# Openings of the four big stages: logarithm straight from PSUM, the norm's steps at higher priority, and two stages' first weights loaded into other buffers

## The chip, the cores and the metric

One core of one Trainium2 chip runs the whole forward pass in one launch. The metric is device time in microseconds (us), the median of several runs. "PE" is TensorE, "DVE" VectorE, "ACT" ScalarE, "POOL" GpSimd, and "SP" is SyncE, whose queue issues the transfers.

## The reference, cut to what matters

Two layers over 512 latent tokens with 256 context tokens ahead of them, width 1024. Layer 0 mixes tokens by grouped-query attention, layer 1 by a bidirectional Mamba-2 SSD; each layer ends in a gated feed-forward network (FFN). Ahead of each of the four sub-layers stands a root-mean-square norm with a shift and a scale:

```
def rms_norm(x, g):
    y = x * lax.rsqrt(jnp.mean(x * x, axis=-1, keepdims=True) + EPS)
    return y * g
def modulate(x, shift, scale):
    return x * (1 + scale) + shift
for i in range(DEPTH):                       # DEPTH = 2
    h = modulate(rms_norm(x, norm_mix_w[i]), ...)
    x = x + gate * (attention_mixer(h) if i == 0 else mamba2_mixer(h))
    h = modulate(rms_norm(x, norm_ffn_w[i]), ...)
    g, u = jnp.split(h @ w_up[i], 2, axis=-1)          # D_FF = 2816
    x = x + gate * ((jax.nn.silu(dwconv(g)) * u) @ w_down[i])
```

## The kernel before, in words

**Products.** Activations lie feature-major: 8 tiles of 128 features by tokens. Every operand of a big product is split into a high part (fp32r, rounded) and a low remainder, and `mm3` (L101 to L111) makes three matmuls of it: high by high (L108), high weight by low activation (L109), low weight by high activation (L111). A weight of 128x1024 is loaded by SP (`load_w`, L96), rounded by ACT (L85, the cast to `wh`) and its remainder taken by DVE (L87, `wl`); the three tiles come from one ring of ten buffers of that size, the tag `t4`, which all stages share.

**Openings.** An opening is the passage from a stage that updates `x` to the stage that reads its norm. The token ranges go one after the other: the context first (where it is still needed), then the first 256 latent tokens (lat0), then the last 256 (lat1). For each range the closing stage updates one feature tile of `x` after another (L874 in `down`, L1284 in `add_out`), and `Norm.sq` squares each on ACT (L338) and adds it up (POOL, for the last tile DVE: L344, L345). When a range is finished, `Norm.gen` makes its norm while the next range's products run: `rstd_rows` sums over the features by matmul (L244, tile `ss`), DVE turns the sums into mean + EPS (L247, `rsa`), ACT takes logarithm and exponential (L249, `rsy`, which is 1/sqrt), DVE corrects them by one Newton step (L251, L252, L254), PE transposes the root across the partitions (L266, `rsT`), and `modulated` forms the eight feature tiles: DVE scales (L294, `ht`), ACT shifts and rounds (L299 and L300, or L303, giving `hh`), and DVE (L304) or POOL (L301) takes the remainder `hl`. Tiles of ffn norms are called `..f`, those of the SSD's norm `..s`.

**First products.** The next stage's first two weights are multiplied by all ranges in `first_tiles`, into two PSUM tiles of tag `S` (`ps_first`; there are two such buffers). Its matmuls on the ranges that are ready run while the last range's norm is being made. For the SSD, `ps_first` holds the projection for the time steps and the first x tile; ACT empties the former (L1007, L1008) and so frees the buffer for the next product, `ps_in`.

**Order.** Apart from the start of attention, whose PE, ACT and DVE orders are written out by hand, a planner fixes each engine's order ahead of the run: it simulates the machine and gives a free engine the ready instruction that was traced first. A transfer or an operation is placed when its buffer is free in that simulation. On the chip each engine then works through its list in that order.

**Pools.** Most tiles that live for one stage come from that stage's own pool (`pa` attention, `pf` first FFN, `pt` SSD, `pg` second FFN), which is closed after the next stage's `first_tiles`; the next pool takes its place in memory. The ten `t4` buffers and the norm's results `hh`, `hl` stand in a pool that is never closed.

Of the kernel before, what the change touches and what calls it, by code (L numbers as in the profile page):

```python
# [7 lines left out]
P = 128  # L8
F32 = mybir.dt.float32
F32R = mybir.dt.float32r  # L10
AF = mybir.ActivationFunctionType
ALU = mybir.AluOpType
# [3 lines left out]
D = 1024  # L16
# [55 lines left out]
def t4(g, name, dt=F32):  # L72
    return g.p.tile([P, 1024], dt, tag="t4", bufs=10, name=name)
# [14 lines left out]
    return cast  # L88


def load_w(g, dram, lo_engine="dve", pin=False, after=None):

    st = t4(g, "wst")
    wh = t4(g, "wh", F32R)
    wl = t4(g, "wl", F32R)
    g.nc.sync.dma_start(st, dram)  # L96
    cast = split(g, st, wh, wl, lo_engine=lo_engine, pin=pin)
    if after:
        behind(g, cast, after)
    return wh, wl  # L100
# [132 lines left out]


def rstd_rows(g, sq, n, cols, width, name, bank):

    nc = g.nc
    c = cols.shape[-1]  # L240
    nt = n // P
    ps = bank(f"ss{name}")
    for t in range(nt):
        nc.tensor.matmul(ps[:, t * c : (t + 1) * c], sq[:, t * P : (t + 1) * P], cols, start=True, stop=True)  # L244
    small = lambda nm: g.p.tile([P, nt * c], F32, tag="rst", bufs=8, name=nm)
    a, y, u = small("rsa"), small("rsy"), small("rsu")
    nc.vector.tensor_scalar(a, ps[:, : nt * c], 1.0 / width, EPS, ALU.mult, ALU.add)  # L247

    for f in ((lambda: nc.scalar.activation(y, a, AF.Ln)), (lambda: nc.scalar.activation(y, y, AF.Exp, scale=-0.5))):  # L249
        follow(g, f()) if g.tables else f()  # L250
    nc.vector.tensor_tensor(u, y, a, ALU.mult)  # L251
    nc.vector.scalar_tensor_tensor(u, y, -0.5, u, ALU.mult, ALU.mult)  # L252
    if c == 1:
        nc.vector.scalar_tensor_tensor(a, u, 1.5, y, ALU.add, ALU.mult)  # L254
        root = lambda t: a[:, t : t + 1].broadcast_to([P, P])
    else:
        rb = t3(g, f"rb{name}", n=n)
        wide = lambda v: v.unsqueeze(2).broadcast_to([P, nt * c, P // c])
        nc.vector.scalar_tensor_tensor(rb.rearrange("p (a b) -> p a b", b=P // c), wide(u), 1.5, wide(y),
                                       ALU.add, ALU.mult)  # L260
        root = lambda t: rb[:, t * P : (t + 1) * P]
    yield BREAK
    for t0 in range(0, nt, 4):
        pt = bank(f"rsT{name}")
        for t in range(t0, min(nt, t0 + 4)):
            nc.tensor.transpose(pt[:, (t - t0) * P : (t - t0 + 1) * P], root(t), g.ident)  # L266
        yield (pt, t0 * P, min(n, (t0 + 4) * P))
# [55 lines left out]
class Norm:  # L323
# [7 lines left out]

    def sq(self, seg, x, m):

        i, a, b = seg
        nc = self.g.nc
        sq = t3(self.g, f"sq{self.name}", n=b - a)
        for ap, c0, c1 in parts(x[i][m], a, b):
            nc.scalar.activation(sq[:, c0:c1], ap, AF.Square)  # L338
        if m in (0, 6):
            self.acc[seg, m] = sq  # L340
            return
        acc = self.acc[seg, 6 if m == 7 else 0]
        if m == 7:
            nc.vector.tensor_tensor(acc, acc, self.acc[seg, 0], ALU.add)  # L344
        (nc.vector if m == 7 else nc.gpsimd).tensor_tensor(acc, acc, sq, ALU.add)  # L345

    def gen(self, seg, x, lag=2):

        i, a, b = seg
        g, nc, n = self.g, self.g.nc, b - a  # L350
        for _ in range(lag):
            yield
        rows = rstd_rows(g, self.acc[seg, 6], n, g.ones[:, :1], D, self.name, lambda nm: Bank(g, nm))
        next(rows)
        for _ in range(lag):
            yield
        rs = next(rows)[0][:, :n]
        for m in range(KT):
            modulated(g, self.h[i][m], x[i], rs, a, b, *self.a, self.streams[i][1], m,
                      pool=m in ((1, 4) if a else (1, 3, 5, 7)))  # L360
            yield


def gemm_in(g, tiles, h, off, segs):


    for run in segs:
        for ps, w in tiles:
            for k in range(KT):
                ks = slice(k * P, (k + 1) * P)  # L370
                mm3(g, (w[0][:, ks], w[1][:, ks]),
                    [(ps[:, off[i] + a : off[i] + b], tuple(t[:, a:b] for t in h[i][k])) for i, a, b in run],
                    k == 0, k == KT - 1)
                yield


def firsts(g, *units):
    return [load_w(g, u) for u in units]
# [507 lines left out]
def ffn(g, layer, streams, x, h, first, nxt=None, side=iter(()), after=()):  # L886

    nc, I = g.nc, g.I  # L890
    ns = len(streams)
    tot = sum(n for n, _ in streams)
    off = [0, L]

    cw = [g.par[:, PC[f"fw{layer}{t}"] : PC[f"fw{layer}{t}"] + NFT] for t in range(3)]
    cb = g.par[:, PC[f"fb{layer}"] : PC[f"fb{layer}"] + NFT]
    whole = [[(i, 0, n) for i, (n, _) in enumerate(streams)]]

    def gemm(t):

        if t % NFT == 0:
            ps = first[t // NFT]
        else:
            w = load_w(g, I["wup"][layer, t])
            if t % NFT == 1:
                out = []
                for i in range(ns):
                    ps = Bank(g, "ps_up1")
                    for _ in gemm_in(g, [(ps, w)], h, (0, 0), [[s] for s in whole[0] if s[0] == i]):
                        pass  # L910
                    out.append((ps, [i]))
                return [(ps[:, : streams[i][0]], off[i], off[i] + streams[i][0], i) for ps, (i,) in out]
            ps = S(g, "ps_up")
            for _ in gemm_in(g, [(ps, w)], h, off, [[s] for s in whole[0]]):
                pass
        return [(ps[:, :tot], 0, tot, None)]

    def up(f):
        pg = gemm(f)
        cv = t3(g, "cv", n=tot)  # L920
        w0, w1, w2 = (c[:, f : f + 1] for c in cw)
        for ps, a, b, _ in pg:
            nc.scalar.activation(cv[:, a:b], ps, AF.Identity, scale=w1, bias=cb[:, f : f + 1])
        for i in range(ns):
            a, b = off[i], off[i] + streams[i][0]
            ps, o = next((ps, o) for ps, o, e, j in pg if j in (None, i))
            nc.vector.scalar_tensor_tensor(cv[:, a + 1 : b], ps[:, a - o : b - o - 1], w0, cv[:, a + 1 : b], ALU.mult, ALU.add)
            nc.vector.scalar_tensor_tensor(cv[:, a : b - 1], ps[:, a - o + 1 : b - o], w2, cv[:, a : b - 1], ALU.mult, ALU.add)
        follow(g, nc.scalar.activation(cv, cv, AF.Silu))
        some = (2, 2, 2, 3)[f] if ns > 1 and f < 4 else 1  # L930
        for _ in range(some):
            next(side, None)
        pu = gemm(NFT + f)
        for _ in range(some):
            next(side, None)
        hd = t3(g, "hd", n=tot)
        for ps, a, b, _ in pu:
            nc.vector.tensor_tensor(hd[:, a:b], cv[:, a:b], ps, ALU.mult)
        hi, lo = t3(g, "hdh", F32R, n=tot), t3(g, "hdl", F32R, n=tot)
        split(g, hd, hi, lo)  # L940
        return [(hi[:, off[i] : off[i] + streams[i][0]], lo[:, off[i] : off[i] + streams[i][0]]) for i in range(ns)]

    gate = g.mod[layer][5]
    segs, f = [], 0
    for n in [3] + [2] * 8 + [3] if nxt else [2] * 11:
        segs.append(range(f, f + n))
        f += n
    acts, pend, wf = {}, None, []

    def flush(fs, order, norm=None, after=None):  # L950
        ws = [load_w(g, I["wdown"][layer, f * P : (f + 1) * P]) for f in fs]
        if after:
            wf.extend(firsts(g, *after))
        return down(g, ws, [acts.pop(f) for f in fs], gate, streams, x, order, norm, side=side)

    for fs in segs:
        for j, f in enumerate(fs):
            acts[f] = up(f)
            if j == 0 and pend:
                flush(pend, whole)  # L960
        pend = fs
    for _ in side:
        pass
    if nxt:
        ln_exp(g)
    return flush(pend, [[s] for s in ending(streams)], nxt, after), wf


def ssd(g, x, norm, wf, bg, close):
# [355 lines left out]
        for seg in SEGS[0]:  # L1325
            nxt.sq(seg, [xn], m)
    wt = [wm(m) for m in (6, 7)]
    wf = firsts(g, I["wup"][1, 0], I["wup"][1, NFT])
    bg = iter(())
    for seg in SEGS[0]:  # L1330
        _, a, b = seg
# [13 lines left out]
def body(nc, tc, I, out, dbg=None):  # L1345
# [21 lines left out]
                             ((CST_IDENT, CST_IDENT + P), (CST_BLK, CST_BLK + 2), (CST_SEL, CST_SEL + 2)))  # L1367
    g.ones = g.const.tile([P, P], F32, name="ones")
    nc.vector.memset(g.ones, 1.0)
    g.sc32 = g.const.tile([P, KT, 32], F32, name="sc32")  # L1370
    nc.vector.memset(g.sc32, 0.0)
    tc.keep_in_program_order(nc.scalar.preload_act_table_set("natural_log_exp_and_others"))
# [157 lines left out]
```

## Time and profile before

| what | us |
|---|---|
| median of 3 runs (1874.18 to 1875.43) | 1875.17 |
| profiled execution, its own time | 1875.38 |
| its span, first to last instruction | 1873.6 |
| PE busy in that span | 1848.9 |
| DVE busy | 1303.6 |
| ACT busy | 807.3 |
| POOL busy | 299.8 |

How to read it: PE is at work nearly all the time, so a change that adds or removes no matmul can move the time only through the stretches in which PE stands still or runs at half clock. The page leaves 1.78 us of the profiled execution outside the span.

### The profile page before, as it was taken

How to read it: one execution, taken by the hardware profiler on the slowest of the kernel's cores; microseconds unless marked ns; L12 is line 12 of the kernel's file. 1: busy time of each engine (PE TensorE's matmuls, PEld its weight loads, DVE VectorE, ACT ScalarE, POOL GpSimd, SP SyncE). 2: the span in 40 equal slices, each digit the busy share in tenths (PEclk: the TensorE clock that was granted, in tenths of full speed). 3: DMA queues.
4: the chain of work that ended last, by engine and by line, in shares of the span. 5: the costliest groups of instructions: out<-in, count | busy, mean ns of one | idle time of the engine just before them, and what ended most of it. 6: DMA issues, size and time to landing. Idle time of an engine off the chain costs nothing.

```text
span 1873.6 us, 28798 instructions
## 1 busy us (share of the span) xinstructions
PE 1848.9 (99%) x11474; PEld 1547.2 (83%) x11474; DVE 1303.6 (70%) x1950; ACT 807.3 (43%) x1402; POOL 299.8 (16%) x266
## 2 busy tenths in 40 slices
PE   9999999999999999999999999999999999999999
PEld 8876656798888888888888888888887888888887
DVE  6588888778787776544487787777797565565655
ACT  4534444363122222222367667776666352323231
POOL 2123120040000000000032333444443210000000
PEclk9999999999999999999999999999999999999999
DMA  9233151124444552211224432443352223222232
GB/s 345 76 109 101 63 178 52 57 84 164 146 135 145 191 185 99 68 58 56 68 91 141 124 105 87 124 124 113 124 178 93 79 91 97 95 95 97 90 103 89
DMA packets 74070, 211.67 MB, mean 113 GB/s; under 512 B 9040, under 2 KB 14544, under 8 KB 73808
## 3 DMA queue, kind: packets, MB, share of 16 engines
q1 hardware_dynamic: 73936, 209.84, 34.0%
q8 instruction: 90, 1.47, 0.3%
q14 instruction: 44, 0.36, 0.1%
HBM read 198.79 MB, written 6.82 MB: 110 GB/s over the span
## 4 chain that ended last, share of the span: by engine, by line
PE 84%; DVE 7%; issue 3%; DMA 2%; POOL 2%; ACT 2%; SPq 0%; DVEq 0%; POOLq 0%; ACTq 0%
PE ps_up L108 10%; PE ps_up L111 10%; PE ps_up L109 10%; PE ps_d L108 6%; PE ps_d L111 6%; PE ps_d L109 6%; PE ps_in L111 4%; PE ps_in L109 4%; PE ps_in L108 4%; PE ps_s L697 2%; PE ps_o L661 2%; PE ps_st L1123 2%; DMA wada<-in_adaA 1%; PE ps_wo L111 1%; PE ps_wo L108 1%
## 5 line engine op out<-in xcount | busy, mean ns | idle before, releaser
L87 DVE TENSOR_TENSOR wl<-wst,wh 128x1024 fp32r<-128x1024 f32 x207 | 258.5, 1249 | 233.9 <-PE ps_up L109 138.9
L85 ACT CAST wh<-wst 128x1024 fp32r<-128x1024 f32 x211 | 221.3, 1049 | 393.7 <-DMA wst<-in_wup 323.6
L108 PE MATMUL ps_up<-hhf,wh 128*128 128x512 f32 x1008 | 357.6, 355 | 0.0
L109 PE MATMUL ps_up<-hlf,wh 128*128 128x512 f32 x1008 | 357.3, 354 | 0.0
L111 PE MATMUL ps_up<-hhf,wl 128*128 128x512 f32 x1008 | 357.0, 354 | 0.0
L108 PEld LDWEIGHTS ps_up<-hhf,wh 128*128 128x128 f32 x1008 | 190.8, 189 | 26.4
L109 PEld LDWEIGHTS ps_up<-hlf,wh 128*128 128x128 f32 x1008 | 190.8, 189 | 26.3
L111 PEld LDWEIGHTS ps_up<-hhf,wl 128*128 128x128 f32 x1008 | 190.6, 189 | 26.4
L108 PE MATMUL ps_in<-hhs,wh 128*128 128x512 f32 (+1 forms) x560 | 204.4, 365 | 1.5 <-ACT dt L1008 1.5
L109 PE MATMUL ps_in<-hls,wh 128*128 128x512 f32 (+1 forms) x560 | 199.4, 356 | 0.0
L111 PE MATMUL ps_in<-hhs,wl 128*128 128x512 f32 (+1 forms) x560 | 198.7, 355 | 0.0
L108 PE MATMUL ps_d<-hdh,wh 128*128 128x512 f32 (+1 forms) x568 | 193.3, 342 | 0.2 <-ACT hdh L85 0.2
L111 PE MATMUL ps_d<-hdh,wl 128*128 128x512 f32 (+1 forms) x568 | 193.5, 341 | 0.0
L109 PE MATMUL ps_d<-hdl,wh 128*128 128x512 f32 (+1 forms) x568 | 192.9, 340 | 0.3 <-DVE hdl L87 0.3
L874 DVE SCALAR_TENSOR_TENSOR X<-ps_d,mod,X 128x512 f32<-128x512 f32 (+1 forms) x224 | 124.3, 583 | 35.9 <-PE ps_d L111 35.2
L108 PEld LDWEIGHTS ps_in<-hhs,wh 128*128 128x128 f32 x560 | 105.9, 189 | 16.6 <-ACT dt L1008 1.7
L109 PEld LDWEIGHTS ps_d<-hdl,wh 128*128 128x128 f32 x568 | 106.7, 188 | 14.8 <-DVE hdl L87 0.7
L111 PEld LDWEIGHTS ps_in<-hhs,wl 128*128 128x128 f32 x560 | 105.8, 189 | 14.7
L111 PEld LDWEIGHTS ps_d<-hdh,wl 128*128 128x128 f32 x568 | 106.6, 188 | 13.1
L108 PEld LDWEIGHTS ps_d<-hdh,wh 128*128 128x128 f32 x568 | 106.3, 188 | 13.4 <-ACT hdh L85 0.7
L109 PEld LDWEIGHTS ps_in<-hls,wh 128*128 128x128 f32 x560 | 106.0, 189 | 13.2
L700 ACT ACTIVATE pr<-ps_s 128x1024 f32<-128x1024 f32 x56 | 57.2, 1021 | 107.2 <-PE ps_s L699 107.2
(339 smaller groups left out, 3653.4 us busy)
## 6 DMA issues: line engine op xcount, KB each, us to landing
wst<-in_wup SPq DMA_DIRECT2D x88, 512.0 KB, 3.3
wada<-in_adaT SPq DMA_DIRECT2D x56, 512.0 KB, 3.3
wst<-in_win SPq DMA_DIRECT2D x48, 512.0 KB, 3.4
wst<-in_wdown SPq DMA_DIRECT2D x44, 512.0 KB, 3.5
E<-ad SPq DMA_DIRECT2D x64, 256.0 KB, 6.9
wada<-in_adaB SPq DMA_DIRECT2D x24, 512.0 KB, 4.1
ec<-ead SPq DMA_DIRECT2D x64, 128.0 KB, 5.6
wst<-in_wout SPq DMA_DIRECT2D x16, 512.0 KB, 3.3
```

What stands on the lines that cost most here:

```text
L85: cast = keep(nc.scalar.copy(hi, src))
L87: keep(eng.tensor_tensor(lo, src, _r(hi), ALU.subtract))
L108: mm(out, wh, ah, start=first, stop=False)
L109: mm(out, wh, al, start=False, stop=False)
L111: mm(out, wl, ah, start=False, stop=last)
L661: nc.tensor.matmul(po[S64[e], :n], v, pr[:, 512 * e + off : 512 * e + off + n], start=first, stop=last)
L697: nc.tensor.matmul(outs[e], kk[e][a][S64[e], k], b[S64[e], q], start=i == 0, stop=False)
L700: exps.append(nc.scalar.activation(pr, ps, AF.Exp))
L874: nc.vector.scalar_tensor_tensor(ap, o[:, c0:c1], gate[:, m, v : v + 1], ap, ALU.mult, ALU.add)
L1123: nc.tensor.matmul(ps[:, d * 256 : (d + 1) * 256], Bt[:, t * P : (t + 1) * P], xw[d][t], start=t == ts[0], stop=t == ts[-1])
```

## The change

1. In `rstd_rows`, ACT takes the logarithm of `sums / width + EPS` straight from the PSUM tile (scale and a constant tile `g.eps` as bias). DVE's mean + EPS is still made, after the two ACT steps in the trace order, for the Newton step. This holds for all norms, those of attention's queries and keys included.
2. In the openings (`Norm`), the square and sum of the last feature tile are traced as if 200 instructions earlier, and everything from the sums to the transposed root as if 400 earlier.
3. The first two weights of the SSD (`flush(..., after)`) go to buffers of the first FFN's pool `pf` that its side work (`ada_dve`) has done with: the three `wada` buffers, `junk` and `cb`. Before, they took `t4` buffers.
4. The first two weights of the second FFN go to `t2` buffers (128x512) of the SSD's pool `pt`, each weight loaded, rounded and split in two halves.
5. `gemm_in` takes a weight's block out of one tile or of a list of two.

```diff
-def load_w(g, dram, lo_engine="dve", pin=False, after=None):
-    st = t4(g, "wst")
-    wh = t4(g, "wh", F32R)
-    wl = t4(g, "wl", F32R)
+def load_w(g, dram, lo_engine="dve", pin=False, after=None, tiles=None):
+    st, wh, wl = tiles or (t4(g, "wst"), t4(g, "wh", F32R), t4(g, "wl", F32R))
+    if isinstance(st, list):
+        for i in range(2):
+            g.nc.sync.dma_start(st[i], dram[:, i * 512 : (i + 1) * 512])
+            split(g, st[i], wh[i], wl[i])
+        return wh, wl
...
-    nc.vector.tensor_scalar(a, ps[:, : nt * c], 1.0 / width, EPS, ALU.mult, ALU.add)
-    for f in ((lambda: nc.scalar.activation(y, a, AF.Ln)), (lambda: nc.scalar.activation(y, y, AF.Exp, scale=-0.5))):
+    sums = ps[:, : nt * c]
+    for f in ((lambda: nc.scalar.activation(y, sums, AF.Ln, scale=1.0 / width, bias=g.eps)),
+              (lambda: nc.scalar.activation(y, y, AF.Exp, scale=-0.5))):
         follow(g, f()) if g.tables else f()
+    nc.vector.tensor_scalar(a, sums, 1.0 / width, EPS, ALU.mult, ALU.add)
...
     def sq(self, seg, x, m):
+        if m < 7:
+            return self.square(seg, x, m)
+        with self.g.tc.high_priority(200):
+            self.square(seg, x, m)
...
-        next(rows)
+        with g.tc.high_priority(400):
+            next(rows)
         for _ in range(lag):
             yield
-        rs = next(rows)[0][:, :n]
+        with g.tc.high_priority(400):
+            rs = next(rows)[0][:, :n]
...
-            wf.extend(firsts(g, *after))
+            part = lambda dt: g.t3p.tile([P, D], dt, tag="wada", bufs=3, name="wada")
+            both = g.t3p.tile([P, 2 * D], F32R, name="cb")
+            wf.append(load_w(g, after[0], tiles=(part(F32), part(F32R), part(F32R))))
+            wf.append(load_w(g, after[1], tiles=(g.t3p.tile([P, D], F32, tag="junk", bufs=1, name="junk"),
+                                                 both[:, :D], both[:, D:])))
...
-    wf = firsts(g, I["wup"][1, 0], I["wup"][1, NFT])
+    two = lambda dt=F32R: [t2("wf", dt) for _ in range(2)]
+    wf = [load_w(g, I["wup"][1, t], tiles=(two(F32), two(), two())) for t in (0, NFT)]
...
+    g.eps = g.const.tile([P, 1], F32, name="eps")
+    nc.vector.memset(g.eps, EPS)
```

More of the change, by code (lines that the diff above doesn't have):

```diff
@@ L332, in sq, with square @@
     def sq(self, seg, x, m):
+        if m < 7:
+            return self.square(seg, x, m)
+        with self.g.tc.high_priority(200):
+            self.square(seg, x, m)
+    def square(self, seg, x, m):
         i, a, b = seg
@@ L369, in gemm_in @@
             for k in range(KT):
-                ks = slice(k * P, (k + 1) * P)
-                mm3(g, (w[0][:, ks], w[1][:, ks]),
+                mm3(g, tuple(parts(v, k * P, (k + 1) * P)[0][0] for v in w),
                     [(ps[:, off[i] + a : off[i] + b], tuple(t[:, a:b] for t in h[i][k])) for i, a, b in run],
```

## The prediction

> **What bounds the kernel now.** I read the page first, then busy time by stage, then PE's waits, and last the timeline around the longest of them.
>
> ```profile
> PE 1848.9 (99%) x11474; PEld 1547.2 (83%) x11474; DVE 1303.6 (70%) x1950; ACT 807.3 (43%) x1402; POOL 299.8 (16%) x266
> L87 DVE TENSOR_TENSOR wl<-wst,wh 128x1024 fp32r<-128x1024 f32 x207 | 258.5, 1249 | 233.9 <-PE ps_up L109 138.9
> L85 ACT CAST wh<-wst 128x1024 fp32r<-128x1024 f32 x211 | 221.3, 1049 | 393.7 <-DMA wst<-in_wup 323.6
> ```
>
> PE is busy 1848.9 of 1873.6 us, and the change takes no matmul away. So 24.7 us of idleness, and time at a lower clock, are all that can be won. The second view has one row per stretch: its start and end, its length, each engine's busy time, the granted clock after POOL's.
>
> ```profile
> core 0: us, PE busy (x) PEld busy (x) DVE busy (x) ACT busy (x) POOL busy (x), PEclk, DMA share, GB/s
> 380.00:425.00 45.00, 43.40 (x328) 41.10 (x328) 35.64 (x78) 28.79 (x63) 16.34 (x20) 1.00 0.29 106
> 925.00:975.00 50.00, 45.95 (x373) 44.09 (x372) 38.10 (x94) 31.46 (x76) 20.50 (x25) 1.00 0.26 92
> 1490.00:1520.00 30.00, 27.19 (x203) 25.66 (x203) 22.57 (x49) 14.97 (x34) 5.13 (x6) 0.94 0.22 74
> 276.32:279.73 3.41, 1.98 (x20) 1.10 (x22) 2.73 (x4) 1.75 (x2) 0.00 (x0) 1.00 0.04 17
> 1508.53:1511.94 3.41, 1.41 (x10) 0.97 (x9) 2.81 (x8) 0.87 (x3) 0.00 (x0) 1.00 0.00 0
> 1511.94:1515.36 3.42, 3.42 (x13) 2.98 (x12) 3.42 (x9) 3.42 (x9) 0.89 (x2) 0.50 0.00 0
> ```
>
> The first three are the openings of the first FFN, the SSD and the second FFN. PE idles 1.6, 4.05 and 2.81 us there, 8.5 together. In the third the clock matters as well: after 3.41 us in which PE was busy for only 1.41, it was granted 0.50 for the next 3.42, which costs half of that, 1.7 us. A stretch of the same length with 1.98 busy stayed at 1.00; so the edge lies between 1.41 and 1.98. The matmuls that wait in the three openings (total, times, longest):
>
> ```profile
> PE ps_first L109 <- POOL hls L301: 1.6, 2, 1.3
> PE ps_first L109 <- POOL hlf L301: 1.5, 2, 1.2
> PE ps_in L108 <- ACT dt L1008: 1.5, 1, 1.5
> PE ps_first L108 <- ACT hhf L303: 1.1, 1, 1.1
> PE rsTf L266 <- DVE rsa L254: 0.9, 1, 0.9
> PE ps_first L109 <- DVE hlf L304: 0.8, 1, 0.8
> ```
>
> First FFN: 1.5. SSD: 1.6 and 1.5. Second FFN: 1.1 + 0.9 + 0.8 = 2.8, and 1.7 for the clock. That makes 9.1 us within reach.
>
> **The change part by part.**
>
> *Second FFN, the last range's norm.* Its chain, from the sums to the first rounded tile:
>
> ```profile
> 1506.36 0.58 PE L244 MATMUL ssf<-ones,sqf 128*128 128x1 f32 x4
> 1506.98 0.16 DVE L247 TENSOR_SCALAR rsa<-ssf 128x2 f32<-128x2 f32 x1 [0.76 <-PE ssf L244]
> 1507.17 0.20 ACT L249 ACTIVATE rsy<-rsa 128x2 f32<-128x2 f32 x1 [1.41 <-DVE rsa L247]
> 1507.28 1.03 ACT L85 CAST wh<-wst 128x1024 fp32r<-128x1024 f32 x1
> 1508.22 0.20 ACT L249 ACTIVATE rsy<-rsy 128x2 f32<-128x2 f32 x1
> 1508.35 1.23 DVE L87 TENSOR_TENSOR wl<-wst,wh 128x1024 fp32r<-128x1024 f32 x1 [1.21 <-ACT wh L85]
> 1509.49 0.15 DVE L251 TENSOR_TENSOR rsu<-rsy,rsa 128x2 f32<-128x2 f32 x1
> 1510.09 0.43 PE L266 MATMUL rsTf<-cst,rsa 128*128 128x128 f32 x2 [0.88 <-DVE rsa L254]
> 1511.07 0.51 ACT L303 ACTIVATE hhf<-ht,mod 128x256 fp32r<-128x256 f32 x1 [2.65 <-DVE ht L294]
> ```
>
> The sums end at 1506.94, and the logarithm starts at 1507.17, when DVE has passed them on; read from PSUM it starts where `rsa` did, at 1506.98: 0.19 saved. Between logarithm and exponential lies a weight's cast, between exponential and Newton step a weight's remainder. Without them the exponential would follow the logarithm's 0.20 at once (0.85 sooner) and the Newton step the exponential's (1509.49 less 1508.42: 1.07 sooner). Together 2.1 us. What the edit does to these two weight steps no row shows: the norm already stands ahead of later weights in the trace order, and they got in because the next norm step was not ready at that instant. Ends: 0.19 won, if they get in again, and 2.1. I take 2.1, because a chain that starts sooner finds the cast's weight not yet landed: the cast ran right in the chain's first gap. PE, out of other work at 1509.2 (1510.09 less 0.88), would then get its first tile at 1511.58 less 2.1 = 1509.5, so 0.4 of the two waits' 2.0 stays: -1.6. With 0.4 idle the 3.41-us stretch is far above 1.98 busy, and the half clock goes: -1.7.
>
> ```profile
> 1502.57 1.46 DVE L87 TENSOR_TENSOR wl<-wst,wh 128x1024 fp32r<-128x1024 f32 x1
> 1503.96 0.96 DVE L304 SCALAR_TENSOR_TENSOR hlf<-ht,mod,hhf 128x256 fp32r<-128x256 f32 x1
> ```
>
> The 0.8 wait is for this remainder of the range before, which stands behind one more weight. An earlier root may bring it ahead of the weight or not; half, -0.4. Second FFN: -3.7.
>
> *The SSD's norm.* Here the lag sits in DVE's and ACT's lists:
>
> ```profile
> 957.37 0.50 PE L244 MATMUL sss<-ones,sqs 128*128 128x1 f32 x4
> 958.66 0.14 DVE L247 TENSOR_SCALAR rsa<-sss 128x2 f32<-128x2 f32 x1
> 958.68 3.43 POOL L301 TENSOR_TENSOR hls<-ht,hhs 128x256 fp32r<-128x256 f32 x3 [2.91 <-ACT hhs L300]
> 959.72 0.19 ACT L249 ACTIVATE rsy<-rsa 128x2 f32<-128x2 f32 x1
> 959.94 0.20 ACT L249 ACTIVATE rsy<-rsy 128x2 f32<-128x2 f32 x1
> 960.74 0.70 DVE L251 TENSOR_TENSOR rsu<-rsy,rsa 128x2 f32<-128x2 f32 x1
> 962.83 0.38 PE L266 MATMUL rsTs<-cst,rsa 128*128 128x128 f32 x2
> ```
>
> From the end of the sums (957.87) to the transposes pass 4.96 us, where the second FFN's chain above needs 3.15 with two weights in it and about 1.05 without. With priority the norm goes ahead of the range before's `ht`, `hh`, `hl` in both lists, so the root comes some 2 to 3 us sooner. Each range gains so, and the remainders on POOL, which PE waits for, with it. Ends: 0, or even a loss where a range's norm pushes back the previous range's remainders, and all 1.6. I take 1.6, since a lead of 2 us is more than the longest wait of 1.3. The first FFN has the same shape: -1.5.
>
> *The SSD's first weights in `pf`: an added wait.* Every access to the SSD's pool waits until `pf` is released:
>
> ```profile
> 969.99 0.47 DVE L304 SCALAR_TENSOR_TENSOR hls<-ht,mod,hhs 128x256 fp32r<-128x256 f32 x1
> 970.62 0.20 ACT L1000 ACTIVATE na<-par 128x1 f32<-128x1 f32 x1 [1.64 <-DVE hls L304]
> 971.56 0.57 ACT L1007 ACTIVATE dte<-ps_first,par 64x384 f32<-64x384 f32 x1 [0.74 <-PE ps_first L111]
> 971.96 0.28 PE L111 MATMUL ps_first<-hhs,wl 128*128 128x256 f32 x1
> 973.10 0.56 ACT L1008 ACTIVATE dt<-ps_first,par 64x384 f32<-64x384 f32 x1
> 973.71 0.38 PE L108 MATMUL ps_in<-hhs,wh 128*128 128x256 f32 x1 [1.47 <-ACT dt L1008]
> ```
>
> L1000 reads only parameters, yet it waits for the last `hl`, the last reader in `pf`. With weights in `pf` the last readers are the `ps_first` matmuls, which end at 972.24. Then come L1000 (0.20) and the four emptying steps (971.56 to 973.66: 2.1), so `ps_in` starts at about 974.6 where it was 973.71: +0.9. Behind L1000 in ACT's list stand the emptying steps, and for them waits PE, which has no other PSUM buffer of that kind. The idle stretch grows to 2.4 us, which leaves some 1.0 busy in 3.41, below the 1.41 that brought the half clock; where the 3.41-us grid cuts it in two, it stays above. I take the drop: +1.7. SSD: -1.6 + 0.9 + 1.7 = +1.0.
>
> By the Trainium skill, page "TensorE: Matmul & The Clock Gate", section "Why this matters for your kernels", the clock falls after idle gaps of over some 3 us. By it the 2.4 us would leave the clock alone, and the sum below would be 1.7 us lower. The rows differ: gaps of 0.88 and about 1.1 us within one 3.41-us stretch brought 0.50.
>
> *The rest.* Weights of the second FFN in `pt`: `pg`'s first tile then waits for the last `ps_first` too, but that only delays work which DVE and ACT (70% and 43% busy) owe PE later, while PE goes on with the next two weights; 0. Halves instead of wholes: between 0 more and, if a half cost as much as a whole, two casts and two remainders more (2 x 1.05 on ACT, 2 x 1.25 on DVE), ahead of the opening, beside 1.4 us or more of DVE slack in every 5; 0 of it on PE, up to 2.5 if that cover were gone. Two more transfers on SP likewise. The `t4` buffers that come free are taken by later weights, so the openings see as many weight steps as now; 0, and this is why I credit nothing to the early loading itself. The logarithm from PSUM in attention's ten norms shortens ACT's stand by some 0.2 us each, beside PE's work: 0. Memset of `g.eps`: 0.
>
> **The sum.** -3.7 - 1.5 + 1.0 = -4.2, against the profiled execution's own 1875.38: 1871.2. That stands 0.21 above the median of the runs, so 1871.0 as a median.
>
> **The rivals.**
> - *No clock drop at the SSD* (grid cuts the stretch, or the page's rule): 1871.0 - 1.7 = 1869.3. For it: the 2.4 us can fall 1.2 by 1.2. Against: the row with 1.41 busy.
> - *Weights slip into the second FFN's chain again*: only 0.19 of its 3.7 is won: 1871.0 + 3.5 = 1874.5. For it: priority cannot help a step that isn't ready, and the planner's clock isn't the chip's. Against: in the SSD's chain the exponential followed the logarithm by 0.03 us.
> - *Priority does nothing to the order* on the chip, and only the pool's wait shows: 1875.2 + 0.9 = 1876.1.
> - *Slower: the pool's wait decides.* Place: `ps_in` after the SSD's first products. Price: 0.9 + 1.7 = 2.6, so 1877.8 if the two FFN openings win nothing. It makes the kernel slower as soon as the three norms win less than 2.6 together. For it: the row of L1000. Against: it needs both FFN norms to stay as they are.
>
> **How the numbers follow.** A difference of 0.2% (3.75 us) is about what a measurement of this kernel tells from none. Chances: forecast 0.45, no drop 0.22, weights slip in 0.18, order unchanged 0.07, pool's wait decides 0.08. The forecast at 1871.0 lies almost on the bound of 1871.4; I count 0.3 of its 0.45 as faster by over 0.2%, the rest as within, and the rival at 1869.3 as faster. The two that end above 1874 count as within, and of the last I give 0.06 to beyond 1878.9 for reorderings in attention and SSD that no row prices. So 0.52 faster, 0.42 within, 0.06 slower. Range: down to all 9.1 won with the pool's wait and no drop (1875.2 - 9.1 + 0.9 = 1867.0), up to 1876.5, which takes in all but the last case; the forecast's own is 1868.5 to 1873.
>
> **What would show it.** Right: in the second FFN's opening no row at 0.50, and L249, L249, L251 one after another; in the SSD's, L266 within 3 us of L244; L1000 waiting for PE `ps_first`; `ps_in` waiting over 2 us for L1008, with 0.50 behind it. Wrong: L1000 still released by DVE; L85 or L87 between L249 and L251; new PE waits in attention or in the SSD's groups.

## The result, and the profile after

The changed kernel took 1886.09 us (median of 4 runs, 1885.67 to 1887.59) beside 1875.30 for the kernel before on the same chip: a ratio of 1.0061, 95% interval 1.0045 to 1.0077 (the ratios in this document are estimated from all runs of both kernels; they are not the quotients of the medians, here 1.0058). The prediction was 1871.0 in a range of 1867.0 to 1876.5, so the time lies outside, on the slower side. The page of the changed kernel:

```profile
span 1884.1 us, 28832 instructions
PE 1850.1 (98%) x11474; PEld 1547.3 (82%) x11474; DVE 1310.6 (70%) x1953; ACT 811.7 (43%) x1404; POOL 287.1 (15%) x266
```

PE's busy time is 1.2 us longer, the span 10.5. So PE stands still more. PE's waits (total, times, longest) say for what. The changed kernel and the experiments have other line numbers: L108, L109, L111 of `mm3` are now L111, L112, L114, the norm's steps lie 3 to 4 lines further down, the SSD's 16.

```profile
PE ps_xt L1113 <- DVE ec L1206: 10.0, 7, 1.9
PE ps_in L111 <- ACT dt L1024: 2.3, 1, 2.3
...
PE rsTf L270 <- DVE rsa L258: 1.5, 1, 1.5
```

The first row is new. `ps_xt` are the transposes of x in the SSD's eight groups of heads, a place that the prediction's sum gives nothing. In the kernel before, the same transposes waited 1.8 us in all, for another step:

```profile
PE ps_xt L1097 <- DVE xf L1200: 1.8, 6, 0.5
```

Two stretches, by window (columns as in the prediction): the groups' projections, from the first `ps_in` to the last, before and after; behind the second of them the openings of first FFN, SSD and second FFN after, and two stretches of 3.41 us out of the groups.

```profile
973.71:1396.81 423.10, 420.48 (x2477) 364.17 (x2478) 323.93 (x376) 291.74 (x617) 152.77 (x133) 1.00 0.39 119
```

```profile
973.89:1407.96 434.07, 422.38 (x2477) 364.90 (x2478) 330.93 (x375) 292.60 (x617) 142.10 (x133) 1.00 0.36 114
380.00:425.00 45.00, 44.41 (x329) 41.74 (x328) 39.72 (x82) 30.76 (x63) 14.60 (x19) 1.00 0.30 109
925.00:975.00 50.00, 45.25 (x363) 42.99 (x364) 38.75 (x93) 30.46 (x75) 18.74 (x25) 1.00 0.22 75
1500.00:1530.00 30.00, 27.23 (x209) 25.95 (x209) 21.89 (x49) 14.21 (x33) 5.85 (x6) 0.94 0.21 71
1225.70:1229.11 3.41, 1.47 (x10) 1.25 (x9) 3.15 (x5) 2.04 (x4) 0.14 (x1) 1.00 0.00 0
1229.11:1232.53 3.42, 3.42 (x10) 2.65 (x9) 1.39 (x2) 1.60 (x3) 1.16 (x2) 0.50 0.00 0
```

The same 2477 matmuls take 434.07 us instead of 423.10. PE idles 11.69 us there (434.07 less 422.38) instead of 2.62. PE's busy time is 1.9 longer, of which 1.7 is the half clock at 1229.11 behind one of the waits. So 11.0 us of loss lie in the groups. The openings moved the time by far less (the table below has them).

One such wait in detail, changed kernel, DVE first and then PE (start, duration, engine, line, tiles, count, idle time before it):

```profile
1052.95 1.21 DVE L87 TENSOR_TENSOR wl<-wst,wh 128x1024 fp32r<-128x1024 f32 x1
1054.08 1.01 DVE L1069 SCALAR_TENSOR_TENSOR Bf<-raw,par,Bf 128x770 f32<-128x770 f32 x1
1055.01 0.68 DVE L1206 TENSOR_TENSOR ec<-ec,ps_yo 128x512 f32<-128x512 f32 x1
```

```profile
1053.20 0.66 PE L1113 MATMUL ps_xt<-cst,xf 128*128 128x128 f32 x4
1055.74 0.66 PE L1113 MATMUL ps_xt<-cst,xf 128*128 128x128 f32 x4 [1.89 <-DVE ec L1206]
1056.15 0.49 PE L111 MATMUL ps_in<-hhs,wh 128*128 128x512 f32 x1
```

and the same place in the kernel before, PE:

```profile
1053.02 0.66 PE L1097 MATMUL ps_xt<-cst,xf 128*128 128x128 f32 x4
1053.43 0.47 PE L108 MATMUL ps_in<-hhs,wh 128*128 128x512 f32 x1
1053.75 0.39 PE L109 MATMUL ps_in<-hls,wh 128*128 128x512 f32 x1
1053.98 0.40 PE L111 MATMUL ps_in<-hhs,wl 128*128 128x512 f32 x1
1054.21 0.60 PE L1097 MATMUL ps_xt<-cst,xf 128*128 128x128 f32 x4
```

Before, PE's list has three `ps_in` matmuls between the first transposes and the second. After, the second transposes stand right behind the first, and the `ps_in` matmuls stand behind them. The first of these could have run: its weight had been cast by 1041.94, and ACT had emptied a PSUM buffer for it by 1053.23. The transposes need a PSUM buffer that DVE empties with `ec`. DVE has a weight's remainder and a convolution tap ahead of `ec`, and PE works in order, so it stands still.

Why the lists differ shows in SP's waits over the groups (985 to 1390 us): what each weight load waited for before it could be issued. Before:

```profile
SPq L96 <- DVE wl L87: 192.8, 29, 14.8
SPq L96 <- PE ps_in L111: 75.1, 12, 8.2
```

After:

```profile
SPq L99 <- PE ps_in L114: 213.2, 31, 13.1
SPq L99 <- PE ps_yo L1204: 42.9, 6, 8.3
SPq L99 <- DVE wl L87: 30.5, 3, 11.3
```

Each weight takes three of the ten `t4` buffers. Before, a load mostly waited for a buffer that DVE had read last; after, mostly for one that PE had read last. The loads, and with them casts and remainders, come at other times in each group. That the planner put the rest around them, and so moved the `ps_in` matmuls, is inferred from the lists; the planner itself left no trace.

### The profile page after: what moved, and what is told of

It is laid out like the page before. It is cut to its first block, busy times and chain, and to the rows that moved or that the text cites. A ratio compares the mean times of both kernels' runs of the same rounds, so it can differ in the third digit from the quotient of the medians.

```text
span 1884.1 us, 28832 instructions
## 1 busy us (share of the span) xinstructions
PE 1850.1 (98%) x11474; PEld 1547.3 (82%) x11474; DVE 1310.6 (70%) x1953; ACT 811.7 (43%) x1404; POOL 287.1 (15%) x266
## 4 chain that ended last, share of the span: by engine, by line
PE 77%; DVE 11%; issue 5%; ACT 3%; DMA 2%; POOL 2%; SPq 0%; POOLq 0%; DVEq 0%; ACTq 0%
PE ps_up L114 10%; PE ps_up L112 10%; PE ps_up L111 10%; PE ps_d L111 6%; PE ps_d L114 6%; PE ps_d L112 6%; PE ps_in L112 2%; PE ps_in L114 2%; PE ps_in L111 2%; PE ps_s L709 2%; DVE xf L1069 2%; PE ps_o L673 2%; DVE Bf L1069 1%; PE ps_wo L111 1%; PE ps_wo L112 1%
## 5 line engine op out<-in xcount | busy, mean ns | idle before, releaser
L87 DVE TENSOR_TENSOR wl<-wst,wh 128x1024 fp32r<-128x1024 f32 x203 | 250.2, 1233 | 306.9 <-PE ps_up L112 142.7
L85 ACT CAST wh<-wst 128x1024 fp32r<-128x1024 f32 x207 | 217.1, 1049 | 417.5 <-DMA wst<-in_wup 321.3
L112 PE MATMUL ps_up<-hlf,wh 128*128 128x512 f32 x1008 | 357.0, 354 | 0.0
L111 PE MATMUL ps_up<-hhf,wh 128*128 128x512 f32 x1008 | 356.9, 354 | 0.0
L114 PE MATMUL ps_up<-hhf,wl 128*128 128x512 f32 x1008 | 356.8, 354 | 0.0
L112 PEld LDWEIGHTS ps_up<-hlf,wh 128*128 128x128 f32 x1008 | 190.6, 189 | 26.4
L111 PEld LDWEIGHTS ps_up<-hhf,wh 128*128 128x128 f32 x1008 | 190.5, 189 | 26.4
L114 PEld LDWEIGHTS ps_up<-hhf,wl 128*128 128x128 f32 x1008 | 190.5, 189 | 26.4
L111 PE MATMUL ps_in<-hhs,wh 128*128 128x512 f32 (+1 forms) x560 | 205.0, 366 | 2.3 <-ACT dt L1024 2.3
L112 PE MATMUL ps_in<-hls,wh 128*128 128x512 f32 (+1 forms) x560 | 199.9, 357 | 0.0
L114 PE MATMUL ps_in<-hhs,wl 128*128 128x512 f32 (+1 forms) x560 | 199.3, 356 | 0.0
L114 PE MATMUL ps_d<-hdh,wl 128*128 128x512 f32 (+1 forms) x568 | 193.6, 341 | 0.0
L112 PE MATMUL ps_d<-hdl,wh 128*128 128x512 f32 (+1 forms) x568 | 193.2, 341 | 0.3 <-DVE hdl L87 0.3
L111 PE MATMUL ps_d<-hdh,wh 128*128 128x512 f32 (+1 forms) x568 | 193.1, 342 | 0.2 <-ACT hdh L85 0.2
L111 PEld LDWEIGHTS ps_in<-hhs,wh 128*128 128x128 f32 x560 | 106.3, 190 | 17.7 <-ACT dt L1024 2.5
L112 PEld LDWEIGHTS ps_d<-hdl,wh 128*128 128x128 f32 x568 | 106.7, 188 | 14.8 <-DVE hdl L87 0.7
L114 PEld LDWEIGHTS ps_in<-hhs,wl 128*128 128x128 f32 x560 | 106.1, 189 | 15.0
L114 PEld LDWEIGHTS ps_d<-hdh,wl 128*128 128x128 f32 x568 | 106.7, 188 | 13.1
L112 PEld LDWEIGHTS ps_in<-hls,wh 128*128 128x128 f32 x560 | 106.4, 190 | 13.5
L111 PEld LDWEIGHTS ps_d<-hdh,wh 128*128 128x128 f32 x568 | 106.3, 188 | 13.4 <-ACT hdh L85 0.6
```

The lines of the kernel that those rows point to most:

```text
L85: cast = keep(nc.scalar.copy(hi, src))
L87: keep(eng.tensor_tensor(lo, src, _r(hi), ALU.subtract))
L111: mm(out, wh, ah, start=first, stop=False)
L112: mm(out, wh, al, start=False, stop=False)
L114: mm(out, wl, ah, start=False, stop=last)
```

## The experiments

Theory A: the SSD's first weights no longer occupy six `t4` buffers, so the SSD's own weights get into the ring earlier and in another step with its buffers, and this sets other lists in the groups. Rivals: B, the pool's wait (which delays the groups' start) upsets them; C, the priorities or the logarithm do.

All runs in one table. The last three columns are stretches of the profiled execution, in us, between starts of matmuls: the SSD's opening (first `ps_first` to first `ps_in`), the groups (first `ps_in` to last `ps_y`), the second FFN's opening (last `ps_y` to its last `ps_first` matmul). The kernel before ran beside each group of experiments: its median was 1874.86 beside e1 to e4, 1874.05 beside e5 to e8, 1874.43 beside e9 to e12.

| kernel | median us | ratio to before (95%) | SSD opening | groups | 2nd FFN opening |
|---|---|---|---|---|---|
| before | | | 28.89 | 452.13 | 94.43 |
| after | 1886.09 | 1.0061 (1.0045-1.0077) | 29.98 | 463.91 | 93.11 |
| e1 SSD weights alone | 1888.45 | 1.0077 (1.0062-1.0092) | 29.43 | 466.13 | 92.84 |
| e2 all but SSD weights | 1874.82 | 0.9998 (0.9989-1.0007) | 27.98 | 452.08 | 93.97 |
| e3 = e2 + pool's wait | 1875.74 | 1.0009 (0.9999-1.0018) | 29.59 | 452.39 | 94.02 |
| e4 after, memsets in `t4` | 1884.95 | 1.0061 (1.0045-1.0078) | 29.72 | 468.60 | 92.50 |
| e5 after, `t4` held | 1873.57 | 0.9995 (0.9985-1.0004) | 27.96 | 452.92 | 93.20 |
| e6 FFN weights alone | 1874.35 | 1.0002 (0.9993-1.0011) | 28.93 | 452.09 | 93.67 |
| e7 logarithm + priorities | 1872.58 | 0.9996 (0.9986-1.0005) | 27.95 | 452.22 | 91.03 |
| e8 logarithm alone | 1874.66 | 1.0004 (0.9994-1.0013) | 29.36 | 452.20 | 90.59 |
| e9 = e2, `t4` held at FFN | 1872.18 | 0.9989 (0.9981-0.9998) | 28.13 | 452.32 | 90.95 |
| e10 e7 + SSD weights, held, no pool's wait | 1876.46 | 1.0008 (0.9999-1.0017) | 27.59 | 456.74 | 91.27 |
| e11 = e10 + FFN weights, held | 1876.29 | 1.0007 (0.9998-1.0016) | 27.59 | 456.14 | 91.35 |
| e12 priorities alone | 1874.90 | 1.0002 (0.9993-1.0011) | 28.93 | 452.14 | 93.89 |

Read the last two columns with the clock in mind: each stretch of 3.41 us at a granted clock of 0.50 lengthens them by up to 1.7. The last column holds one such stretch in before, after, e2 and e3, and none in the others; the groups hold one in after and e5, two in e4, e10 and e11, three in e1.

**e1 and e2: the SSD's weights alone, and all but them.** In e1 the rest of the change is undone; in e2 only this:

```diff
-            part = lambda dt: g.t3p.tile([P, D], dt, tag="wada", bufs=3, name="wada")
...
+            wf.extend(firsts(g, *after))
```

e1:

> The kernel before with one part of the change: the SSD's first two weights in pf instead of the t4 ring; logarithm, priorities and second FFN's weights as before. Theory A (six free t4 buffers let the SSD's own weights come earlier, so other steps stand in DVE's and PE's lists in its eight groups): the groups lose the 10 to 11 us that they lost in the full change, and nothing is won at the FFNs' openings: 1875.3 + 0.9 (the pool's wait) + 10.5 = about 1886.7, with ps_xt waiting for ec some 7 times, 10 us in all. Theory B (the pool's wait, which starts the groups 0.9 us later, upsets them): the same here. Theory C (the priorities or the logarithm upset the groups): 1875.3 + 0.9 = 1876.2, ps_xt waiting 2 us or less.

e2:

> The full change without that one part: the SSD's first weights stay in the t4 ring. Theories A and B: the groups run as before; what was won ahead of them and behind them in the full change stays: first FFN -1.5, second FFN's opening about -1.4, and no pool's wait (-0.7 by the start of ps_in): 1872 to 1873.5. Theory C: ps_xt still waits 10 us for ec, 1884 to 1886.

e1 lost the whole amount and a little more: groups 466.13 us, with the same row among PE's waits (`ps_xt` for `ec`, 10.4 us, 7 times). The little more goes with the clock: 0.50 for three stretches in e1's groups, for one in the changed kernel's. e2's groups took 452.08. Theory C falls. e2 was not the 1872 to 1873.5 that I expected but 1874.82; in the second FFN's opening it won 0.5 us, where e7 without the early weights won 3.4 (below).

**e3: the pool's wait alone.**

```diff
     ps_dt, ps_x0 = first_tiles(g, wf, norm, bg)
+    nc.vector.tensor_copy(g.t3p.tile([P, 1], F32, name="last"), ps_x0[:, T - 1 : T])
```

> The kernel of e2 with only the pool's wait put back: a DVE step of one element reads the last column of ps_first into a tile of pf before pf is released, so that the SSD's pool waits until the last ps_first matmul has ended, while the weights stay in t4. Theory A: ps_in starts 0.9 to 1.2 us later than in e2 and nothing else moves: e2 + 1, 1873 to 1874.5, ps_xt as before (about 2 us of waits). Theory B: the groups lose their 10 us: 1884 to 1886.

The SSD's opening grew by 1.6 us against e2 (27.98 to 29.59), the time by 0.9, which is within the noise; the groups stayed at 452.4. Theory B falls: the wait costs something in the opening and upsets nothing in the groups.

**e4 and e5: the buffers taken, and held.** Both are the full change. e4 takes six buffers for a memset each; e5 keeps them until the SSD's last `ps_first` (the added statements, each on a line of its own):

```diff
 # e4, in ssd, behind close()
+    [nc.gpsimd.memset(t4(g, "pad")[:, :1], 0.0) for _ in range(6)]
 # e5, in flush, behind the two loads
+            g.hold = [t4(g, "hold") for _ in range(6)]
+            [nc.gpsimd.memset(t[:, :1], 0.0) for t in g.hold]
 # e5, in ssd, behind first_tiles
+    [nc.vector.tensor_tensor(t[:, :1], t[:, :1], ps_x0[:, T - 1 : T], ALU.add) for t in g.hold]
```

e4:

> The full change, with six t4 buffers taken once (one memset of one column each on POOL, 6 x 0.1 us) where the SSD's weights would have taken them, behind the release of pf, so that the SSD's own weights come no earlier than before. Theory A: the groups' 10 to 11 us are gone, and the pool's wait is left: 1873 to 1875. Theory B and C: 1885 to 1887.

e5:

> The full change, with six t4 buffers held as long as the SSD's first weights held them before: six memsets of one column on POOL where those weights were loaded, and six DVE steps of one column behind the last ps_first. (In e4 each buffer was free again as soon as its memset had run, so e4 didn't hold them.) Theory A (the free buffers let the SSD's own weights come early, which sets the order of the eight groups): the groups run as in e3, without waits for ec; with the six steps and the pool's wait 1875 to 1877. Theory F (the order hangs on something else in that part, the pool pf's later end or the weights' own place): ps_xt waits 10 to 13 us for ec, 1884 to 1887.

e4 was a miss: 468.60 us in the groups, `ps_xt` waiting 13.1 us. Its buffers were free again as soon as each memset had run, so it did not hold back what theory A says must be held back; by itself it would also have fitted theory F. SP's timeline shows it. Counted from the SSD's first `ps_first`, the SSD's own first two weights are issued 8.5 and 11.0 us after it in the kernel before, 30.3 and 22.0 us ahead of it in the changed kernel, and 29.3 and 21.9 ahead in e4. In e5 they come 8.3 and 10.4 us after it, as before, and e5 decides. With everything else of the change in place the groups took 452.92 us, the time fell from 1886 to 1873.6, and the transposes' waits, and in the same window as above SP's, are nearly those of the kernel before:

```profile
PE ps_xt L1113 <- DVE xf L1216: 1.8, 6, 0.5
```

```profile
SPq L99 <- DVE wl L87: 192.4, 29, 14.8
SPq L99 <- PE ps_in L114: 82.0, 13, 8.3
```

So the loss hangs on when the six buffers come free. One rival is weakened but not excluded: the hold's small steps stand in the planner's lists too, and no run has those steps without the hold. Against it speak e4, whose six memsets turned nothing, and e9 below, where a hold works at another place. e5 shows a second thing. The stretch from the SSD's first to its last `ps_first` took 25.35 us, where after took 27.37 and e7, without the early weights, 27.28. Only with the buffers held did the early weights bring their 2 us there. The time does not show them: 1873.57 beside 1874.05 is within the noise.

**e6 and e7: what takes the gain at the second FFN.** e6 is before with the second FFN's weights in `pt` alone; e7 is the change with both pairs of weights back in `t4`.

> The kernel before with the second FFN's first two weights alone loaded early, in halves, in pt. Theory D (these free buffers put the norm's sums and its transposes close together in PE's list, ahead of the ps_wo products that could fill the gap): rsTf waits 1.5 us, with the clock at 0.5 behind it, and nothing else changes: 1875 to 1876.5. Theory E (the raised priority of the transposes does that): rsTf waits 0.9 us or less here, 1874 to 1875.

> The change's logarithm and priorities, with both pairs of first weights in the t4 ring as before. Theory D: rsTf waits 0.9 us or less, no row at 0.5 in the second FFN's opening, and its other waits are shorter by the priority: e2's 1874.8 less 1.5 to 3, 1872 to 1873.3. Theory E: rsTf waits 1.5 us as in e2, 1874.5 to 1875.

e7's opening took 91.03 us, e2's 93.97; the only difference there is the early weights. In the changed kernel one sees how they cost it. PE:

```profile
1506.00 0.50 PE L247 MATMUL ssf<-ones,sqf 128*128 128x1 f32 x4
1506.36 0.36 PE L112 MATMUL ps_wo<-yl,wh 128*128 128x256 f32 x1
1506.56 0.28 PE L114 MATMUL ps_wo<-yh,wl 128*128 128x256 f32 x1
1508.34 0.43 PE L270 MATMUL rsTf<-cst,rsa 128*128 128x128 f32 x2 [1.50 <-DVE rsa L258]
1508.53 0.36 PE L111 MATMUL ps_wo<-hhy,wh 128*128 128x256 f32 x1
```

and the 3.41-us stretches around it:

```profile
1505.60:1509.01 3.41, 1.91 (x17) 1.71 (x17) 1.58 (x8) 1.42 (x3) 0.00 (x0) 1.00 0.48 177
1509.01:1512.43 3.42, 3.42 (x19) 3.42 (x18) 3.42 (x9) 2.98 (x8) 0.80 (x2) 0.50 0.16 61
```

The first range's transposes stand two matmuls behind their sums, and the `ps_wo` products that could fill the 1.5 us stand behind the transposes; a half clock followed, another 1.7. e6 has the same wait, 1.3 us, without any priority, and e7 none with all of them. So it is theory D, not the priorities (E), that holds, although e6 had no row at 0.50 and lost nothing in all. Of the 2.9 us between e2 and e7 in this opening 1.7 are the half clock and 1.3 idle time of PE.

**e8: the logarithm alone**, and **e12: the priorities alone.**

> Logarithm from PSUM alone. By the prediction's terms 0 in attention and 0.2 to 0.4 in the second FFN: 1874.5 to 1875. Theory G (attention's norms are in PE's way, since in the three kernels of this study with the logarithm attention's scores took 247.6 to 247.8 us from the first to the last, where before had 248.7): attention a further 0.9 shorter, 1873.5 to 1874.

> The priorities alone. By the difference of e7 and e8: ps_in starts 0.7 us behind the SSD's last ps_first (before 1.75, e8 1.99), and nothing elsewhere; by the prediction 1.6 us for the SSD and 1.5 for the first FFN's opening (55.94 us from attention's last scores to the last ps_first before; 55.24 in e7, 56.22 in e8: 0.7 so far): 1 to 2 us under before. In the second FFN, where e8 alone has 90.59 us against 94.43: about 94 if the logarithm did all of it there.

e8's chain in the second FFN's last range:

```profile
1507.80 0.26 ACT L251 ACTIVATE rsy<-ssf,eps 128x2 f32<-128x2 f32 x1 [1.22 <-PE ssf L247]
1508.09 0.20 ACT L252 ACTIVATE rsy<-rsy 128x2 f32<-128x2 f32 x1
1508.20 1.03 ACT L85 CAST wh<-wst 128x1024 fp32r<-128x1024 f32 x1
```

```profile
1508.09 0.16 DVE L254 TENSOR_SCALAR rsa<-ssf 128x2 f32<-128x2 f32 x1 [1.05 <-ACT rsy L251]
1508.36 0.16 DVE L255 TENSOR_TENSOR rsu<-rsy,rsa 128x2 f32<-128x2 f32 x1
```

The cast stands behind the exponential, no remainder ahead of the Newton step: the chain that the prediction drew, and the opening fell from 94.43 to 90.59. Of these 3.8 us 1.7 are the half clock and 1.75 idle time of PE (3.20 before, 1.45 in e8). In e12 the half clock is gone too, but PE idles 3.50 us and the opening fell by 0.5 only. So in the profiles the logarithm did it alone. e12 also missed its forecast elsewhere: `ps_in` starts 1.87 us behind the last `ps_first`, not 0.7, and nothing was won in all.

By the timing both kernels are level with before: e8's interval, 0.9994 to 1.0013, leaves room for a gain of 1.1 us at most. The profiled execution of e8 was the fastest of its ten (1872.75 beside a median of 1874.66), and over all runs its mean granted clock was 0.9985, where the kernel before had 0.9986: it did not have fewer half clocks. A half clock that is missing from one profile is no gain of the kernel.

**e9 to e11: the buffers held at the second FFN too, and the pool's wait removed.** e9 is e2 with a hold as in e5, behind the second FFN's weights, read behind its `first_tiles`. e10 is e7 with e5's early SSD weights and hold, and with edits of which these are the main lines, so that nothing ahead of `ps_in` touches `pt`; two of the six held buffers take the first results of the time step's emptying. e11 adds e9's part:

```diff
-    na = small("na", [P, 1])
+    na = g.const.tile([P, 1], F32, name="na")
...
+    e0, r0 = (t[:, :TH] for t in g.hold[:2])
...
-        nc.scalar.activation(e[hs], src, AF.Abs, bias=par("dtb", 0)[hs])
-        nc.scalar.activation(dt[hs], src, AF.Relu, bias=par("dtb", 0)[hs])
+        nc.scalar.activation(e0[hs], src, AF.Abs, bias=par("dtb", 0)[hs])
+        nc.scalar.activation(r0[hs], src, AF.Relu, bias=par("dtb", 0)[hs])
```

> The kernel of e2 (logarithm, priorities, second FFN's weights early) with six t4 buffers held until the second FFN's last ps_first, by six one-column memsets on POOL and six one-column DVE steps. In e2 the stretch from the SSD's last ps_y to the second FFN's last ps_first took 93.97 us, in e7 without the early weights 91.03. Theory A (it is again the freed t4 buffers, filled by later weights whose steps move the opening's order): 91 or less, rsTf waits 0.6 us or less, e2 less 3: some 1.5 us under before. Theory H (the halves, or pt as their place, cost it): 93.5 to 94, as e2.

> Logarithm, priorities and the SSD's first weights in pf, with six t4 buffers held as in e5; two of the six are used for the first results of the time step's emptying (dte, dt), and na lies in the const pool, so that nothing in front of ps_in waits for pf. Second FFN's weights as before. e5's opening (25.35 us from the SSD's first to its last ps_first, where e7 took 27.28) with e7's 0.7 us to ps_in (e5: 2.61): 1.9 us less than e7, some 3.5 us under before. If the pool's wait isn't what the 2.61 is, 0 against e7.

> e10 with the second FFN's weights early too and their six buffers held as in e9: by theory A e10's time less up to 1.5 us (the opening of the second FFN without its weight steps), some 4 to 5 us under before; by theory H 3 us more than e10.

e9 bore out theory A a second time: 90.95 us for the opening instead of 93.97, and the only ratio of the study whose interval lies below 1 (0.9981 to 0.9998). Its median is 2.2 us under before. That is weak evidence for a gain: it is one interval out of thirteen, it just misses 1, and it overlaps e7's (0.9986 to 1.0005). e7 without early weights took 91.03 in that opening, so the early weights themselves add nothing. e10 and e11 were misses. With the pool's wait gone, PE waited for the weight instead:

```profile
970.36 0.38 PE L111 MATMUL ps_in<-hhs,wh 128*128 128x256 f32 x1 [2.98 <-ACT wh L85]
973.69 0.58 PE L114 MATMUL ps_in<-hhs,wl 128*128 128x256 f32 x1 [2.82 <-DVE wl L87]
```

The cast of that weight ran at 969.27, behind the emptying of `ps_first`: 5.8 us of new waits. They also cost clock:

```profile
969.30:972.71 3.41, 0.50 (x2) 0.30 (x2) 3.27 (x3) 2.89 (x4) 0.00 (x0) 1.00 0.00 0
972.71:976.12 3.41, 2.43 (x11) 2.43 (x12) 3.31 (x7) 0.00 (x0) 0.00 (x0) 0.50 0.00 0
976.12:979.54 3.42, 3.42 (x16) 3.23 (x15) 3.31 (x5) 0.00 (x0) 0.00 (x0) 0.50 0.00 0
```

With 2.43 us of PE busy in the first stretch at 0.50, the loss to the clock is 1.2 there and 1.7 in the second. The mean granted clock of e10's runs is 0.9962 where the kernel before has 0.9986, so this is not the profiled execution alone. e10 came out at 1876.46, e11 at 1876.29.

## Why the prediction was wrong, step by step

*The step that failed* is in "The rest": "The `t4` buffers that come free are taken by later weights, so the openings see as many weight steps as now; 0". The sentence was true and the price wrong: it looked at the openings alone, while the ring serves the groups too. Later weights did take them, and the SSD's opening gained nothing by the early ones (27.37 us to its last `ps_first`, e7 27.28). But the loads then followed the ring in another step through all eight groups, and there the term measured +11.8 us (463.91 less 452.13): 9.1 of idle time and 1.9 of busy time up to the last `ps_in`, 0.8 behind it. The prediction's text has the groups only as "0.06 to beyond 1878.9 for reorderings in attention and SSD that no row prices", and among its signs of being wrong, "new PE waits in attention or in the SSD's groups", which is the sign that came. A view that bore on it was there before the change: SP's waits, with 29 loads in the groups held up by DVE's remainders. The change touched just what they wait for. Why the planner's two patterns each keep themselves up through eight groups, no run here shows.

*The gains were too large as well.* The measured median lies 15.1 us above the forecast, and in the profiles the groups make up 11.8 of them. The rest are gains that did not come. For the logarithm and the priorities alone the prediction's terms give -3.7 - 1.5 - 1.6 = -6.8. That is e7, whose median lies 1.5 under before, with an interval of 0.9986 to 1.0005, so 2.6 us at most. (e7's profiled execution is 4.4 us shorter than before's from the first scores to the last matmul, 1754.4 for 1758.8; that this is near the sum of -4.2 is chance, since -4.2 also holds the early weights, which e7 lacks.)

*Second FFN, -3.7.* In the profiles the logarithm alone brings the two things that the prediction named, shorter waits and no half clock: -3.8 in e8, -3.4 in e7. But 1.7 of that is the half clock of one profiled execution, and e8's timing shows no gain, so the size is not borne out. In the change 2.9 of it went again (e2 against e7), for which the prediction had no term: the early weights were to cost 0. "Halves" and "`pg`'s first tile" were not the reason, since e9, with both, has 90.95. Two smaller slips in the working move nothing: 1509.5 less 1509.2 leaves 0.3 us of waiting, not 0.4, and the DVE slack of 1.4 us in every 5 holds for 1380 to 1490 us (1.5) but not for 1490 to 1504 (0.9).

*First FFN, -1.5.* PE's idle time in the window fell from 1.6 to 0.6 us, so -1.0; by the matmuls' starts, from attention's last scores to the last `ps_first`, 55.94 became 55.22. Right in kind, half to two thirds of the size; the priorities did it (54.91 in e12, 56.22 in e8).

*SSD's norm, -1.6.* Wrong. From the end of the sums to the transposes passed 4.96 us before. With the priorities, e12:

```profile
957.95 0.61 PE L247 MATMUL sss<-ones,sqs 128*128 128x1 f32 x4 [0.35 <-DVE sqs L356]
963.47 0.43 PE L270 MATMUL rsTs<-cst,rsa 128*128 128x128 f32 x2 [0.30 <-DVE rsa L258]
```

963.47 less 958.56, the end of the sums, is 4.91: nothing won. e7's DVE list shows why: between two steps of the chain, each of which waits for ACT's or its own last result, a ready step slips in.

```profile
959.21 0.67 DVE L256 SCALAR_TENSOR_TENSOR rsu<-rsy,rsu 128x2 f32<-128x2 f32 x1
959.80 1.21 DVE L87 TENSOR_TENSOR wl<-wst,wh 128x1024 fp32r<-128x1024 f32 x1
960.94 0.70 DVE L258 SCALAR_TENSOR_TENSOR rsa<-rsu,rsy 128x2 f32<-128x2 f32 x1
```

The prediction had that argument ("priority cannot help a step that isn't ready") for the second FFN, where it wasn't needed, and not here, where it was. What logarithm and priorities did win here together lies elsewhere: `ps_in` starts 0.67 us behind the last `ps_first` in e7, where it was 1.75 before; neither part alone brought it (1.99 in e8, 1.87 in e12).

*The pool's wait, +0.9.* Right against the kernel before: from the last `ps_first` to `ps_in` 1.75 us became 2.61. Against e2, which has 0.68 there, it is 1.9, since the wait also took back what the other parts had won. In the changed kernel L1016, the old L1000, waits for `ps_first` as foretold, and `ps_in` 2.33 us:

```profile
971.64 0.20 ACT L1016 ACTIVATE na<-par 128x1 f32<-128x1 f32 x1 [3.14 <-PE ps_first L114]
```

*Clock drop there, +1.7.* It fell out: the stretch was cut by the grid, as the rival at 1869.3 had it (1.85 and 2.63 us of PE busy; the rows are in the last section). The grid can be worked out from the rows: in the changed kernel the half clocks begin at 1229.11 and 1509.01, 279.90 us or 82 times 3.413 apart, and 973.11 lies 75 times 3.413 ahead of 1229.11. In e5 the same 2.3 us fell into one stretch, 1.08 us of PE busy, and brought 0.50:

```profile
969.18:972.59 3.41, 1.08 (x10) 1.08 (x10) 2.39 (x16) 3.25 (x8) 0.00 (x0) 1.00 0.56 189
972.59:976.01 3.42, 3.42 (x19) 3.42 (x18) 3.11 (x3) 3.20 (x6) 0.00 (x0) 0.50 0.30 121
```

By the Trainium skill, page "TensorE: Matmul & The Clock Gate", section "Why this matters for your kernels", the clock falls after idle gaps of over some 3 us. The rows differ, as those of before did: here it fell after a wait of 2.3 us, and at the second FFN after one of 1.5.

*The SSD's sum, +1.0,* came out by luck. The SSD's opening grew by 1.1 us in the profiles (28.89 to 29.98), but of the three terms -1.6, +0.9 and +1.7 only the middle one was there.

*Attention, 0.* The ten profiles with the logarithm need 247.6 to 248.9 us from the first scores to the last, the four without it 248.7, 249.0, 250.3 and 250.4. The slowest of the ten (e9) and the last two of the four (e1, e12) hold a half clock there. With 1.7 taken off for it, the ten lie at 247.2 to 248.1 and the four at 248.6 to 249.0. So the logarithm seems to win somewhat under a microsecond, for which the prediction had 0; the medians don't show it.

*The rival on the slower side* named the wrong place: the pool's wait cost its 0.9 and did not decide the time.

## What to carry to other kernels

Buffers set free are a change to every stage that shares their ring, not only to the one that gave them up: ask first what each later load waits for (the DMA queue's own waits), and allow for lists made by a planner to settle into another pattern. Here that pattern cost 11.8 us. Loading early without taking up a shared ring can be tried with the ring's buffers held for as long as before, which here turned 1886 into 1873.6 us. Raising the priority of a chain moves steps that are ready; the gaps between its dependent steps are still filled by others. And when two profiles differ by a half clock, look at the granted clock of all runs before counting it as won or lost.

## What the runs showed of the hardware that was not expected

The edge that the prediction drew for the clock, between 1.41 and 1.98 us of PE busy in a 3.41-us stretch, is no sharp one in this view. A stretch with 1.91 (1505.60, above) was followed by 0.50, and in the same run this one with 1.85 was not:

```profile
969.70:973.11 3.41, 1.85 (x17) 1.66 (x15) 0.60 (x8) 1.46 (x4) 0.00 (x0) 1.00 0.02 5
973.11:976.52 3.41, 2.63 (x22) 2.63 (x23) 1.75 (x4) 3.36 (x8) 0.00 (x0) 1.00 0.00 0
```

So the busy time of a stretch does not decide by itself; what else does, these rows do not show. A single wait of 1.5 us was enough once (1505.60). Where the grid lies matters too, and it differed among these kernels: the pool's wait of 2.3 us brought the half clock in e5 and not in the changed kernel, where the grid cut it in two. Two stretches at 0.50 followed one with only 0.50 us of PE busy (969.30 in e10, above).
